# Where operands lie in SBUF: places of weight sets, turned probabilities and raw weights in a one-layer encoder

## The chip, the cores and the metric

The kernel runs on one core of a Trainium2 chip. The metric is the device time of one execution in microseconds. Three runs of the kernel before took 1039.4, 1039.71 and 1041.84 us; the median is 1039.71.

## The reference

One layer of an encoder works on 512 tokens of width 1024, in float32: a SwiGLU feed-forward block (width 2816), two attention mixers side by side on one normalised input, and a second SwiGLU block. Each of the three has an RMSNorm ahead of it, and shift, scale and gate come from a conditioning vector `c`.

```python
mod = c_act @ w_mod[l] + b_mod[l]
h = modulate(rmsnorm(x, norm_ffn1[l]), sh1, sc1)
x = x + 0.5 * g1 * swiglu(h, w_ffn1_in[l], w_ffn1_out[l])
h = modulate(rmsnorm(x, norm_mix[l]), sh2, sc2)
qa, ka, va, qb, kb, vb, ga, gb = split(h @ w_in[l])
ya = window_gqa_sink(rope(norm(qa)), rope(norm(ka)), va, sink_a) @ w_branch_a[l]
yb = (rmsnorm(diff_attention(qb, kb, vb, lam)) * 0.8) @ w_branch_b[l]
x = x + g2 * ((sigmoid(ga) * ya + sigmoid(gb) * yb) @ w_out[l])
h = modulate(rmsnorm(x, norm_ffn2[l]), sh3, sc3)
x = x + 0.5 * g3 * swiglu(h, w_ffn2_in[l], w_ffn2_out[l])
```

Mixer A is attention in a window of 128 with a sink; mixer B takes the difference of two softmaxes.

## The kernel before

**Precision.** Each float32 matrix is split into a high part in float32r and a low part, the remainder (`split_from`, L189: ScalarE copies, VectorE subtracts). A product is three matmuls, high x high, high x low, low x high (`mm3`, L173 to L175; `two`, L456 to L458, for halves of 256 tokens). Activations lie with features on the partitions, tokens along them.

**Weight sets.** Weights stream from HBM. A load lands in a raw tile (512 KB, 1024 elements per partition), is split into one of `HILO` = 5 sets in the tiles `high` and `low`, and the matmuls read it from there. `high_low` (L193 on) hands out the sets in turn. Set i begins at element i x 1024 + min(i, 2) x GAP + `aside` of the two tiles; a set that a holder still needs is passed over. The aside shifts a set by a few elements: 0, `ASIDE` (16), `TURN` (24) or `FAR` (64), chosen where the load is written.

**SBUF.** Tiles are laid one behind the other in the order in which their tags first appear: the scratch of the DMA descriptors, small tiles, `x`, `high`, `mod` columns, `low`, `begin`, `ka`, twelve `b8` tiles of 8 KB per partition, more `mod` columns, six `u4` tiles of 4 KB, `pos`, five `raw` tiles of 4 KB, eight `f2` tiles of 2 KB.

**The stages.** Up to about 61 us: loads, the first norm, the modulation and the first four blocks of the first feed-forward product. Then two blocks with 512-column matmuls, and the others in units (`Unit`, L460 on): seven products of 256 columns where plain halves take eight, with sums of operands (`n1`, `n2`, `t3`, `t4`) and sums of weights made by accumulating DMAs from the POOL queue. A set of such a unit is 24 matmuls. `n1` of both feed-forward blocks lies in u4 tiles, the other sums in b8 tiles. The output of the first block comes in four chunks (`Out1`) of 512-column matmuls between the units; its last four rows of blocks run in halves of 256 tokens (`by_halves`) in `boundary`, beside which the next norm and the first three gates run. These three gates have their weights in u4 tiles (`spare`).

From about 377 to 700 us the mixers run. A planner (`Line`) puts pieces of the attentions, each with a due time from a written cost, between the main stream's matmuls: `project` for vb, kb, qb, `gates`, `project_pairs` for the a projections (there the weights are streamed and `hh`, `hl` are what is loaded), more gates, then `branch` for w_yb and w_ya. In the attentions the probabilities are turned by TensorE (`turned`), split into u4 tiles (`diff_turn`, `window_turn`) and multiplied with the values as loaded operand. `load_main` fetches a set through a raw tile: SP issues the load, ScalarE makes the high copy and a negated one, and POOL adds the weights to the latter by an accumulating DMA. `load_halves` splits with `split_from`. w_out follows (`MIX_ASIDES`), then `in_unit` and `out_unit` for the second feed-forward block: a plain unit, a leading unit that runs beside it, and the others in a written order (`items`), with the two out units of a part behind each group; of an out unit the sets run as s1, a11, a12, s2, s4, s3, a22, with the set a22 of the unit before between s1 and a11.

**Order.** Inside `manual_schedule` and in the units the order on each engine is the written one; elsewhere the tile planner picks by priority. SP and POOL issue transfers in order, so a transfer that waits for its tile holds up those behind it.

Of the kernel before, what the change touches and what calls it, by code (L numbers as in the profile page):

```python
# [98 lines left out]

ASIDE, TURN, GAP = 16, 24, 64  # L100

FAR = 64


BRANCH_ASIDES = (ASIDE, TURN, ASIDE, ASIDE), (ASIDE,) * 4
MIX_ASIDES = 0, 0, 0, 0, 0, 0, ASIDE, ASIDE

# [26 lines left out]
def layer(ctx: ExitStack, tc: tile.TileContext, a: dict):  # L134
# [13 lines left out]
    def xt():  # L148
        return sbuf("x", [P, T], F32, 8)
# [7 lines left out]
    def u4(dt=F32R):  # L157
        return sbuf("u4", [P, 2, T], dt, 6)
# [7 lines left out]
    def keep(shape, nm, dt=F32):  # L166
        return sb.tile(shape, dt, name=nm, tag=nm, bufs=1)
# [28 lines left out]
    def high_low(n=1024, aside=0, holder=None):  # L196
        while turn[0] % HILO in holders:
            turn[0] += 1
        i = turn[0] % HILO
        turn[0] += 1  # L200
        if holder:
            holders[i] = holder
        i = i * 1024 + min(i, 2) * GAP + aside
        return tuple(t[:, i : i + n] for t in parts)
# [27 lines left out]
    rqa, ccol = keep([P, NT, 8], "rqa"), small(NC)  # L232
    x = [xt() for _ in range(NC)]
    parts, modv = [], []
    for nm, n in (("high", 6), ("low", 0)):
        parts.append(keep([P, HILO * 1024 + 2 * GAP + ASIDE], nm, F32R))
        modv += [keep([P, NC], f"mod{v}") for v in range(n)]
# [13 lines left out]

    begin, begins, norms = keep([P, 6 * NC], "begin"), {}, {SC1: NORM1, SC2: NORM2, SC3: NORM3}

# [206 lines left out]
    class Unit:  # L460
# [14 lines left out]

        in_order = turned = by_columns = ()
        spare, roomy, apart, more = ("s1",), (), (), {"s1": ("s2", "a11"), "s2": ("s4", "a12"), "a11": ("s3", "a21")}
# [16 lines left out]
        def prepare(self, q):  # L494

            if q in self.ready:
                return
            self.ask(q)
            n = self.depth * 2 * P
            if q in self.apart:  # L500
                both = b8().rearrange("p a b -> p (a b)")
                hi, lo = both[:, 0:n], both[:, 1024 : 1024 + n]
            else:
                hi, lo = high_low(n, TURN if q in self.turned else ASIDE, (self, q))
            t = self.at[q]
            with tc.issue_after(copied[0]) if q in self.in_order and copied else nullcontext():
                split_from(hi, lo, t)
            self.ready[q] = hi, lo
            if q in self.more:
                s, src = self.more[q]  # L510
                G.dma_start(t, self.srcs[src], accum_op=ALU.add)
                self.at[s] = t
# [104 lines left out]
    hh, hl = new_h()  # L617
    modv += [keep([P, NC], f"mod{v}") for v in range(len(modv), 9)]
    nc.scalar.dma_start(ccol, a["c"])
    tc.keep_in_program_order(nc.scalar.dma_start(par, a["par"]))  # L620
# [3 lines left out]
    with tc.manual_schedule(engines=BOUND | {mybir.EngineType.SP, mybir.EngineType.Pool}):  # L624
# [24 lines left out]
        def first_loads(k):  # L649
            n = 1 if k else 2  # L650
            scale = mod_load(SC1, k, n=n)
            if k == 0:
                kept.append(keep([P, NT], "pos", I32))
            shift = mod_load(SH1, k, n=n) if k == 0 else None
            raw = sbuf("raw", [P, 1024], F32, RAW)
            load_by(raw, a["w1s"][k], n)
            w1[k] = [scale, shift or mod_load(SH1, k), raw]
# [227 lines left out]
    def in_unit1(p):  # L885
        srcs = {q: a["w1u"][p - PLAIN, i] for i, q in enumerate(("a11", "a12", "a21", "a22"))}
        u = Unit(srcs, 4, h1_operand, in_post1, p % 2)
        u.p, u.in_order = p, ('s2', 's4')
        return u

    class Out1:
# [17 lines left out]
        def prepare(self, m):  # L909
            if m not in self.ready:  # L910
                self.ask(m)
                aside = FAR if not self.by_halves(m) else TURN if m < NC - LAST_1 + 2 else ASIDE
                if self.final and m == 0:
                    while turn[0] % HILO != 1:
                        turn[0] += 1
                t = self.ready[m] = high_low(self.depth * P, aside, (self, m))
                with tc.issue_after(copied[0]):
                    split_from(*t, self.at[m])
# [196 lines left out]
    def load_main(src, aside=0):  # L1115

        raw = sbuf("raw", [P, 1024], F32, RAW)
        nc.sync.dma_start(raw, src)
        hi, lo = high_low(aside=aside)
        halves = slice(0, 512), slice(512, 1024)  # L1120
        for j in halves:
            S.copy(hi[:, j], raw[:, j])
        for j in halves:
            S.activation(lo[:, j], raw[:, j], AF.Identity, scale=-1.0)
        G.dma_start(lo, src, accum_op=ALU.add)
        return hi, lo


    def load_halves(src, aside=0):
        raw = sbuf("raw", [P, 1024], F32, RAW)  # L1130
        hi, lo = high_low(aside=aside)
        nc.sync.dma_start(raw, src)
        for j in (slice(0, 512), slice(512, 1024)):
            split_from(hi[:, j], lo[:, j], raw[:, j])
        return hi, lo
# [61 lines left out]

    def project_pairs(srcs, then):

        n = 2 * P  # L1200
        out = [bank("acc") for _ in range(2)]
        for u, src in enumerate(srcs):
            wh, wl = load_main(src, ASIDE)
            for t in range(NT):
# [22 lines left out]
    def gates(more=lambda: True):  # L1227
        while gate_next[0] < 16 and more():
            j = gate_next[0]
            gate_next[0] += 1  # L1230

            wh, wl = load_main(a["w_gate"][j], ASIDE * (j == EARLY_A))
            out = bank("acc")
# [152 lines left out]
    def diff_turn(h, b, p):  # L1386
# [4 lines left out]
        if i == 0:  # L1391
            pair = [u4().rearrange("p a b -> p (a b)") for _ in range(2)]
            pt_b[g] = [t.rearrange("p (k i q) -> p k i q", k=NT, i=2) for t in pair]
# [228 lines left out]
    def window_turn(b, g, kc, sc):  # L1622
        tag = turn_tag(b, g, kc)
        tp = turned([sc[q][:, kc * P : (kc + 1) * P] for q in (0, 2, 1, 3)], tag)
        pt = u4()
        with tc.high_priority():
# [37 lines left out]

    def branch(w, j0, o_h, o_l, then, load, r=FULL[0], asides=(0, 0, 0, 0)):
        for u in range(4):
# [13 lines left out]
    def main():  # L1680
# [6 lines left out]
        tables_a()  # L1687
        yield from project_pairs([a["w_kva"][u] for u in range(2)], keys_a)
        for g in range(2):
# [22 lines left out]
        for i, r in enumerate(HALVES):  # L1712
            line.drain(lambda: done["a"] >= 2 * i + 2)
            yield from branch(a["w_ya"], 0, *wa["o"], then_b, load_halves, r, BRANCH_ASIDES[i])

# [87 lines left out]
    def out_unit(part, g, final):  # L1803
# [10 lines left out]
        srcs = {q: a["w2o"][g, i][:, r] for i, q in enumerate(("a11", "a12", "a21", "a22"))}  # L1814
        return Unit(srcs, len(part), act_operand, post, g)

# [23 lines left out]
    plain = units[0] = Plain(units[0].srcs, 4, h_operand, None, 0)  # L1840
    plain.turned = ("a11", "a21")
    lead = units[1]
    lead.spare, lead.roomy, lead.apart = ("s1", "a11", "a12"), ("a22",), ("s1", "a12")
    for u in units[1:]:
        u.in_order = ("s2", "s3", "s4", "a22") if u is lead else ("s1", "s2", "s3", "s4", "a22")
    units[2].MAKE = {**Unit.MAKE, "s2": 3}
    lead.tags = {"w": "acc", "v": "tp"}
    with tc.manual_schedule(engines={mybir.EngineType.Pool}):
# [250 lines left out]
```

## Time and profile before

| | |
|---|---|
| median of three runs | 1039.71 us |
| the profiled execution, its own time | 1039.97 us |
| its span in the profile | 1038.2 us |
| TensorE busy | 1030.8 us, 99%, 7346 matmuls |
| weight loads, VectorE, ScalarE, GpSimd busy | 951.1, 786.9, 583.9, 162.5 us |
| granted clock of TensorE | 1.0 in every slice |

In groups of instructions a row gives line, engine, operation, output and inputs (the first input of a matmul is what is streamed, the second what is loaded, buffer numbers left out), shape, count, busy time and the mean duration of one in ns. Matmuls are pipelined: one of 256 columns lasts about 276 ns, but the next starts after some 113 ns. In a timeline the first column is the start in us, the second the duration.

### The profile page before, as it was taken

The numbers are of one execution on the slowest core, as the hardware profiler recorded it, in microseconds if no ns is written. First come the engines' busy times: TensorE is split into PE (matmuls) and PEld (weight loads), VectorE is DVE, ScalarE is ACT, GpSimd is POOL, SyncE is SP. The second block draws the span as 40 slices with busy tenths as digits, with TensorE's granted clock in tenths as the row PEclk, the third lists the DMA queues.
The fourth block names the chain that finished last, engine by engine and source line by source line (L and its number), as shares of the span: only waits on it lengthen the run. The fifth ranks groups of instructions, "written<-read, shape, count | busy, mean of one in ns | idle before, by whom it ended". The sixth has DMA issues, their size and how long they took to land.

```text
span 1038.2 us, 18851 instructions
## 1 busy us (share of the span) xinstructions
PE 1030.8 (99%) x7346; PEld 951.1 (92%) x7346; DVE 786.9 (76%) x1456; ACT 583.9 (56%) x1014; POOL 162.5 (16%) x190
## 2 busy tenths in 40 slices
PE   9999999999999999999999999999999999999998
PEld 7789899899999998899888888989999999999998
DVE  7786667567796679859782598976899777877877
ACT  6665335244364343667785856525867546654553
POOL 1101110110110100543333101001112112112210
PEclk9999999999999999999999999999999999999999
DMA  9977787966884459796737944974498998989974
GB/s 360 356 238 203 233 231 209 257 166 205 253 203 133 152 192 410 236 288 139 186 69 190 254 134 151 364 252 104 94 237 191 243 229 207 224 223 214 211 156 112
DMA packets 70377, 220.92 MB, mean 213 GB/s; under 512 B 8464, under 2 KB 13200, under 8 KB 70288
## 3 DMA queue, kind: packets, MB, share of 16 engines
q1 hardware_dynamic: 47808, 146.52, 39.0%
q0 software_dynamic: 19344, 68.70, 35.9%
q10 hardware_dynamic: 3136, 4.51, 1.2%
q8 instruction: 57, 0.93, 0.3%
q14 instruction: 32, 0.26, 0.1%
HBM read 209.46 MB, written 10.23 MB: 212 GB/s over the span
## 4 chain that ended last, share of the span: by engine, by line
PE 94%; DMA 2%; DVE 2%; ACT 2%; issue 0%; SPq 0%; DVEq 0%; ACTq 0%
PE acc L457 7%; PE acc L458 7%; PE acc L456 7%; PE sc L457 6%; PE sc L458 6%; PE sc L456 6%; PE sc L173 5%; PE sc L174 5%; PE sc L175 5%; PE acc L173 5%; PE acc L175 5%; PE acc L174 5%; PE tp L1270 2%; DMA raw<-w1s 2%; PE acc L1192 2%; PE acc L1194 2%
## 5 line engine op out<-in xcount | busy, mean ns | idle before, releaser
L189 ACT CAST high<-raw 128x1024 fp32r<-128x1024 f32 (+2 forms) x176 | 158.2, 913 | 152.9 <-PE sc L174 40.4
L189 DVE TENSOR_TENSOR low<-raw,high 128x1024 fp32r<-128x1024 f32 (+2 forms) x176 | 183.2, 1050 | 42.1 <-ACT high L189 40.8
L456 PE MATMUL acc<-b,high 128*128 128x256 f32 x508 | 140.9, 277 | 0.0
L457 PE MATMUL acc<-b,high 128*128 128x256 f32 x508 | 140.7, 277 | 0.1
L458 PE MATMUL acc<-b,low 128*128 128x256 f32 x508 | 140.6, 277 | 0.0
L457 PE MATMUL sc<-b,high 128*128 128x256 f32 x500 | 138.2, 276 | 0.0
L456 PE MATMUL sc<-b,high 128*128 128x256 f32 x500 | 138.1, 276 | 0.0
L458 PE MATMUL sc<-b,low 128*128 128x256 f32 x500 | 138.1, 276 | 0.0
L189 ACT CAST high<-u 128x1024 fp32r<-128x1024 f32 (+1 forms) x73 | 75.5, 1035 | 50.5 <-PE sc L174 20.2
L189 DVE TENSOR_TENSOR low<-u,high 128x1024 fp32r<-128x1024 f32 (+1 forms) x73 | 87.6, 1200 | 20.4 <-ACT high L189 18.8
L173 PE MATMUL sc<-b,high 128*128 128x512 f32 (+1 forms) x272 | 97.5, 358 | 0.0
L174 PE MATMUL sc<-b,high 128*128 128x512 f32 (+1 forms) x272 | 97.2, 357 | 0.0
L175 PE MATMUL sc<-b,low 128*128 128x512 f32 (+1 forms) x272 | 97.1, 357 | 0.0
L457 PEld LDWEIGHTS acc<-b,high 128*128 128x128 f32 x508 | 95.5, 188 | 0.4 <-DVE b L1883 0.3
L456 PEld LDWEIGHTS acc<-b,high 128*128 128x128 f32 x508 | 95.5, 188 | 0.3 <-ACT f L534 0.2
L458 PEld LDWEIGHTS acc<-b,low 128*128 128x128 f32 x508 | 95.4, 188 | 0.0
L458 PEld LDWEIGHTS sc<-b,low 128*128 128x128 f32 x500 | 93.9, 188 | 0.0
L456 PEld LDWEIGHTS sc<-b,high 128*128 128x128 f32 x500 | 93.9, 188 | 0.0
L457 PEld LDWEIGHTS sc<-b,high 128*128 128x128 f32 x500 | 93.9, 188 | 0.0
L173 PE MATMUL acc<-b,high 128*128 128x512 f32 (+1 forms) x240 | 89.0, 371 | 0.0
L175 PE MATMUL acc<-b,low 128*128 128x512 f32 (+1 forms) x240 | 86.7, 361 | 0.0
L174 PE MATMUL acc<-b,high 128*128 128x512 f32 (+1 forms) x240 | 86.5, 361 | 0.0
(397 smaller groups left out, 2715.9 us busy)
## 6 DMA issues: line engine op xcount, KB each, us to landing
u<-w_mod SPq DMA_DIRECT2D x38, 512.0 KB, 8.3
b<-w_mod SPq DMA_DIRECT2D x32, 512.0 KB, 5.5
raw<-w2i SPq DMA_DIRECT2D x31, 512.0 KB, 5.4
u<-w2i POOLq DMA_DIRECT2D x31, 512.0 KB, 6.7
raw<-w1u SPq DMA_DIRECT2D x24, 512.0 KB, 7.1
u<-w1u POOLq DMA_DIRECT2D x24, 512.0 KB, 7.1
raw<-w1o SPq DMA_DIRECT2D x24, 384.0 KB, 4.4
raw<-w_gate SPq DMA_DIRECT2D x16, 512.0 KB, 5.2
```

The lines of the kernel that those rows point to most:

```text
L173: PE.matmul(out, wh, xh, start=first, stop=False)
L174: PE.matmul(out, wh, xl, start=False, stop=False)
L175: PE.matmul(out, wl, xh, start=False, stop=last)
L189: last = S.copy(hi, src), V.tensor_tensor(lo, src, f(hi), ALU.subtract)
L456: PE.matmul(out, wh[:, s], xh, start=first and j == 0, stop=False, skip_group_check=True)
L457: PE.matmul(out, wh[:, s], xl, start=False, stop=False, skip_group_check=True)
L458: PE.matmul(out, wl[:, s], xh, start=False, stop=last and j == 1, skip_group_check=True)
L1192: PE.matmul(out[t][:, 0:n], hh[k][:, ht], wh[:, o : o + n], start=k == 0, stop=False)
L1194: PE.matmul(out[t][:, 0:n], hl[k][:, ht], wh[:, o : o + n], start=False, stop=k == NC - 1)
L1270: PE.transpose(tp[:, j * P : (j + 1) * P], src, ident)
```

## The change

It moves operands within SBUF and swaps two kinds of tiles; no matmul, no split and no transfer is added or removed.

- `high_low`: every set is followed by GAP (64 elements), and 16 elements are added to every aside. `TURN` goes; `FIRST` = -8 and `ENTRY` = 32 are new.
- Two unused tiles, `pad1` (48 elements) ahead of `high` and `pad2` (40) ahead of u4; `begin` and `pos` become longer. The descriptor scratch shrinks from 4096 to 2048 bytes, since the sets take more.
- Single sets stand at FIRST: the first set behind an Out1 chunk or at the start of the units, one of the last w_out sets, units[2]'s a11, s1 of the first out unit of a part (not the last part), the first w_ya set. In project_pairs the first set has aside 8 (-FIRST), the others -16. Of the last Out1 rows in halves the first stands at ENTRY.
- Gates from `EARLY_A` (5) on have aside -16.
- `load_main`, and `load_halves` where it is given an aside (w_ya), take their raw weights into u4 tiles; the turned probabilities of both attentions go into raw tiles.

```diff
-ASIDE, TURN, GAP = 16, 24, 64
+ASIDE, FIRST, GAP = 16, -8, 64
+ENTRY = 32
-BRANCH_ASIDES = (ASIDE, TURN, ASIDE, ASIDE), (ASIDE,) * 4
-MIX_ASIDES = 0, 0, 0, 0, 0, 0, ASIDE, ASIDE
+MIX_ASIDES = 0, 0, 0, 0, 0, 0, FIRST, ASIDE
...
-        i = i * 1024 + min(i, 2) * GAP + aside
+        i = i * (1024 + GAP) + ASIDE + aside
...
+    keep([P, 48], "pad1")
-        parts.append(keep([P, HILO * 1024 + 2 * GAP + ASIDE], nm, F32R))
+        parts.append(keep([P, HILO * (1024 + GAP) + ASIDE], nm, F32R))
...
-    begin, begins, norms = keep([P, 6 * NC], "begin"), {}, {SC1: NORM1, SC2: NORM2, SC3: NORM3}
+    begin, begins, norms = keep([P, 6 * NC + ASIDE], "begin"), {}, {SC1: NORM1, SC2: NORM2, SC3: NORM3}
...
-                hi, lo = high_low(n, TURN if q in self.turned else ASIDE, (self, q))
+                hi, lo = high_low(n, self.asides.get(q, ASIDE), (self, q))
...
+    keep([P, 40], "pad2")
...
-                kept.append(keep([P, NT], "pos", I32))
+                kept.append(keep([P, 2 * NC], "pos", I32)[:, 0:NT])
...
+        if p == PLAIN:
+            u.asides = {"s1": FIRST}
+        elif 2 * p in [c.start for c in CHUNKS[1:]] or p == PLAIN + 1:
+            u.asides = {"s2": FIRST}
...
-                aside = FAR if not self.by_halves(m) else TURN if m < NC - LAST_1 + 2 else ASIDE
+                aside = (ENTRY if m == NC - LAST_1 else ASIDE) if self.by_halves(m) else FAR
...
     def load_main(src, aside=0):
-        raw = sbuf("raw", [P, 1024], F32, RAW)
+        raw = u4(F32).rearrange("p a b -> p (a b)")
...
-    def load_halves(src, aside=0):
-        raw = sbuf("raw", [P, 1024], F32, RAW)
+    def load_halves(src, aside=None):
+        if aside is None:
+            raw, aside = sbuf("raw", [P, 1024], F32, RAW), 0
+        else:
+            raw = u4(F32).rearrange("p a b -> p (a b)")
...
-            wh, wl = load_main(src, ASIDE)
+            wh, wl = load_main(src, -FIRST if first else -ASIDE)
+            first = False
...
-            wh, wl = load_main(a["w_gate"][j], ASIDE * (j == EARLY_A))
+            wh, wl = load_main(a["w_gate"][j], -ASIDE if j >= EARLY_A else 0)
...
-            pair = [u4().rearrange("p a b -> p (a b)") for _ in range(2)]
+            pair = [sbuf("raw", [P, 1024], F32R, RAW) for _ in range(2)]
...
-        pt = u4()
+        pt = sbuf("raw", [P, 1024], F32R, RAW).rearrange("p (a b) -> p a b", a=2)
...
-            yield from branch(a["w_ya"], 0, *wa["o"], then_b, load_halves, r, BRANCH_ASIDES[i])
+            yield from branch(a["w_ya"], 0, *wa["o"], then_b, load_halves, r, (ASIDE if i else FIRST,) + (ASIDE,) * 3)
...
-        return Unit(srcs, len(part), act_operand, post, g)
+        u = Unit(srcs, len(part), act_operand, post, g)
+        if g == 0 and not final:
+            u.asides = {"s1": FIRST}
+        return u
...
-    plain.turned = ("a11", "a21")
...
+    units[2].asides = {"a11": FIRST}
...
-    nc = bacc.Bacc("TRN2", target_bir_lowering=False, num_devices=1, dynamic_dma_scratch_size=4096)
+    nc = bacc.Bacc("TRN2", target_bir_lowering=False, num_devices=1, dynamic_dma_scratch_size=2048)
```

More of the change, by code (lines that the diff above doesn't have):

```diff
@@ L474, in layer @@
         asked, length = ("s1", "a11", "a12", "a22"), 1.0
-        in_order = turned = by_columns = ()
+        in_order, by_columns, asides = (), (), {}
         spare, roomy, apart, more = ("s1",), (), (), {"s1": ("s2", "a11"), "s2": ("s4", "a12"), "a11": ("s3", "a21")}
@@ L1196, in project, with project_pairs @@
         then(out)
-    def project_pairs(srcs, then):
+    def project_pairs(srcs, then, first=False):
         n = 2 * P
@@ L1662, in window_out, with branch @@
             turns["w"] = (b, g * nk + kc + 1)
-    def branch(w, j0, o_h, o_l, then, load, r=FULL[0], asides=(0, 0, 0, 0)):
+    def branch(w, j0, o_h, o_l, then, load, r=FULL[0], asides=(0,) * 4):
         for u in range(4):
@@ L1687, in main @@
         tables_a()
-        yield from project_pairs([a["w_kva"][u] for u in range(2)], keys_a)
+        yield from project_pairs([a["w_kva"][u] for u in range(2)], keys_a, True)
         for g in range(2):
```

## The prediction

> **What bounds the kernel now.** I read the page's busy times first, then what TensorE waited for, then the groups of its instructions by form, over the run and in short windows.
>
> ```profile
> span 1038.2 us, 18851 instructions
> PE 1030.8 (99%) x7346; PEld 951.1 (92%) x7346; DVE 786.9 (76%) x1456; ACT 583.9 (56%) x1014; POOL 162.5 (16%) x190
> PEclk9999999999999999999999999999999999999999
> ```
> ```profile
> PE acc L703 <- ACT b L690: 2.1, 2, 1.7
> PE acc L631 <- DVE sm L637: 0.9, 1, 0.9
> PE tp L728 <- DVE f L718: 0.5, 1, 0.5
> PE acc L186 <- DVE u L189: 0.2, 1, 0.2
> ```
>
> TensorE is busy 99% at the full granted clock, and the second view says that in the whole run it waited 3.7 us for other engines, all but 0.2 us of it before the long stream begins. So the time is the number of matmuls times their spacing, and an edit counts only if it changes the spacing or makes a new wait. The change touches no matmul: their number and shapes stay. What it moves is where operands lie. I call the byte address of an operand modulo 256 its place, worked out from the order and sizes of the allocations: b8 and ka at 64, u4 at 160, raw and f2 at 192, the weight sets (high, low) at 64 plus four times the aside, so 128 with ASIDE, 160 with TURN. The distance is the place of the weights that are being loaded minus that of the operand that is streamed meanwhile. First, does the spacing depend on it? Two windows of the same instructions at the same places (weights 128, b8 at 64, distance 64), before and after a short stop at 315.5 us; columns are window, length, busy time and (x) those reaching into it:
>
> ```profile
> 298.90:315.40 16.50, 16.50 (x148) 1.00 0.71 169
> 316.00:323.40 7.40, 7.40 (x65) 1.00 0.54 159
> ```
> ```profile
> L456 PE MATMUL acc<-b,high 128*128 128x256 f32 x62 | 17.1, 276 | 0.0
> ```
> ```profile
> L457 PE MATMUL acc<-b,high 128*128 128x256 f32 x22 | 6.2, 281 | 0.0
> ```
>
> About 2.4 more reach into a window than start in it, so the spacing is 16.50/145.6 = 113.3 ns before the stop and 7.40/62.6 = 118.2 ns after it. The mean of one (276 in the window 797.5 to 825, 281 in 316.2 to 323.4) moves by the same 5 ns. So mean ns above 276 is a price per 256-column matmul, and distance 64 has two paces, a quick one and a slow one, that last until something disturbs them. The other distances, each a group by form:
>
> ```profile
> L458 PE MATMUL acc<-u,low 128*128 128x256 f32 x80 | 22.4, 280 | 0.0
> ...
> L457 PE MATMUL acc<-u,high 128*128 128x256 f32 x80 | 22.3, 279 | 0.0
> L456 PE MATMUL acc<-u,high 128*128 128x256 f32 x80 | 22.3, 279 | 0.0
> ...
> L457 PE MATMUL sc<-u,high 128*128 128x256 f32 x72 | 20.1, 280 | 0.0
> L458 PE MATMUL sc<-u,low 128*128 128x256 f32 x72 | 20.1, 280 | 0.0
> L456 PE MATMUL sc<-u,high 128*128 128x256 f32 x72 | 20.1, 279 | 0.0
> ```
> ```profile
> L456 PE MATMUL acc<-b,high 128*128 128x256 f32 x8 | 2.2, 281 | 0.0
> ```
> ```profile
> L456 PE MATMUL acc<-b,b 128*128 128x256 f32 x8 | 2.3, 283 | 0.0
> ```
>
> The 456 with u4 (distance 224) cost 3 to 4 ns each. The fourth group is the 24 that follow the 512-column matmuls of an Out1 (window 142.56 to 145.3): distance 64 in its slow pace. The last is distance 0: 7 ns.
>
> **The change part by part.** The new layout, by the same arithmetic: the scratch gives back 2048 bytes, a multiple of 256; pad1 puts high and low at place 0, GAP between all sets keeps each there, pad2 puts u4 at 64, the longer pos puts raw and f2 at 128; b8 and ka stay at 64. A set then stands at 64 (aside 0), 128 (ASIDE), 32 (FIRST), 192 (ENTRY) or 0 (-ASIDE). Pads, begin and pos issue nothing and cost nothing.
>
> 1. The u4 operands get distance 64. Now 80 x (4+3+3) + 72 x (4+4+3) = 1.59 us. Of these the PLAIN unit's 24 in s1 and 48 in s1 of two out units stand at place 32, distance 224 as now, 72 x 3.5 = 0.25. I take the quick pace for the rest, since the window 797.5 to 825 and its like hold it for long. Saved: **1.34**. At worst they run at 281 and 0.5 is lost.
>
> 2. The three leading sets after an Out1 go from 281 to the 280 of distance 224: 72 x 1 = **0.07**; the u4 set behind them, counted in 1, no longer has to disturb the slow pace.
>
> 3. In project_pairs the weights are what is streamed, and hh and hl are loaded.
>
> ```profile
> L1211 PE MATMUL acc<-high,b 128*128 128x256 f32 x21 | 5.9, 280 | 0.0
> L1213 PE MATMUL acc<-high,b 128*128 128x256 f32 x21 | 5.9, 279 | 0.0
> ```
> These 288 (window 455 to 462, distance 192) go to distance 64, the first set to 224: between 0 (slow pace, no better) and 288 x 3.3 = 0.95. Transposes and scores break in here, and after a break either pace may come, so I take a third: **0.3**.
>
> 4. Turned probabilities, with vb or vz as the weights (window 500 to 645):
>
> ```profile
> L175 PE MATMUL acc<-b,low 128*128 128x512 f32 x119 | 46.8, 393 | 0.0
> L174 PE MATMUL acc<-b,high 128*128 128x512 f32 x119 | 46.6, 392 | 0.0
> ...
> L175 PE MATMUL op<-u,b 128*128 128x256 f32 x64 | 18.1, 282 | 0.0
> L174 PE MATMUL op<-u,b 128*128 128x256 f32 x64 | 18.0, 281 | 0.0
> ```
> In raw (place 128) they get distance 192, whose rows are those of point 3: 216 x (281.5 - 279.5) = **0.43**. Ends: 0, and 216 x 5.5 = 1.19 if distance 192 has a quick pace too.
>
> 5. The 11 gates from EARLY_A on, 264 matmuls of 512 columns, go from distance 0 to 192, which no 512-column row shows. The undisturbed ones at distance 0 (window 377 to 428), and those at distance 64 (502.2 to 506.6):
>
> ```profile
> L1192 PE MATMUL acc<-high,b 128*128 128x512 f32 x58 | 22.6, 389 | 0.0
> ```
> ```profile
> L174 PE MATMUL acc<-b,high 128*128 128x512 f32 x7 | 2.8, 395 | 0.0
> ```
> Now they take 392.5 in the attention (389 only in long runs). Ends: 264 x 3.5 = 0.92 gained, 264 x 2.5 = 0.66 lost. 392.5 itself lies about midway, so I take **0**.
>
> 6. The boundaries (windows 340 to 377 and 701 to 746.2).
>
> ```profile
> L174 PE MATMUL acc<-b,u 128*128 128x256 f32 x48 | 13.5, 280 | 0.0
> ```
> ```profile
> L174 PE MATMUL sc<-b,high 128*128 128x256 f32 x48 | 13.4, 280 | 0.0
> ```
> ```profile
> L456 PE MATMUL sc<-b,high 128*128 128x256 f32 x40 | 11.1, 278 | 0.0
> ...
> L174 PE MATMUL sc<-b,high 128*128 128x256 f32 x32 | 9.0, 280 | 0.0
> ```
> The first three gates' weights in u4 come to distance 0 from 96: 144 x (283 - 280) = 0.43 **lost**. The last Out1 and w_mix (144 and 96 at 280) get one set at 192 or 32 and the rest at 128; after stops both paces occur, so of 240 x 4 = 0.96 I take a quarter, 0.24. FFN2's plain unit leaves TURN: of 120 x 2 = 0.24 half, 0.12; w_ya the same kind, 0.05. Together **0.0**.
>
> 7. Buffers. w_gate, w_yb, w_kva, w_qa and w_ya now pass through u4 (6 tiles, shared with the a tables, the mask and mod columns), the probabilities through raw (5 tiles, with the b tables until the keys and queries are done). SP issues in order: behind a load that waits for a u4 tile stand the next weights and the gate_scr reads, for which TensorE and then DVE wait. Past the start TensorE waits 0.2 us in all (the fourth row of the second view), so sets arrive ahead of their use now, and that lead covers the swap; I take 0. If it is gone, each late set shows as a wait of TensorE for high or low. No row shows what the halved scratch could hold back; the transfers that POOL issues make TensorE wait nowhere now, so 0.
>
> Sum: 1.34 + 0.07 + 0.3 + 0.43 + 0 + 0 = 2.1 us. The profiled run took 1039.97, so 1037.9; the median, 1039.71, lies 0.26 lower: about **1037.6**.
>
> **The rivals.** *The quick pace holds almost everywhere*: points 1 (1.34), 2, 3 (0.95), 4 (1.19), 5 (0.92), 6 (0.7 instead of 0), and the 65 behind the stop (0.3): 5.4 us, 1034.3; half of what is open gives 1036. For it: the quick pace once found lasts for hundreds of matmuls. Against: distance 0 shows no quick one at 256 columns. *Nothing*: the excess belongs to what went before (512 columns, stops), not to places; points 3 to 5 at their low ends and u4 at 281 give -0.5 to +1.3 us, 1038.4 to 1040.2. The Trainium skill is on this side: TensorE: Matmul & The Clock Gate, Step-by-step, gives the streamed and the loaded operand two independent read ports, and SBUF — State Buffer, SBUF: two separate sides, says TensorE never waits on anyone. By that every distance would cost alike and the time would stay 1039.7; the 276, 280 and 283 above disagree. *Slower*: the u4 sets were what threw the slow pace off again. With nearly all of FFN2 at distance 64, one stop puts it there until the next set at 32. The last two of these are s1 of the first out unit of a group; s2, which begins with operands in ka, is the fourth set after it, 4 x 24 x 113.3 ns = 10.9 us later:
>
> ```profile
> 824.80 0.28 PE L456 MATMUL acc<-ka,high 128*128 128x256 f32 x1
> ```
> ```profile
> 939.55 0.28 PE L456 MATMUL acc<-ka,high 128*128 128x256 f32 x1
> ```
> So they stand near 814 and 929 us. Between them lie 1014 matmuls, behind the second up to 1034 us 930: at 4.9 ns 5.0 and 4.6 us. Both lost give 1047.2; it decides from 1060 slow ones, (2.1 + 3.1)/0.0049. For it: the stop at 315.5. Against: at the same instructions now the quick pace lasts. *Earlier start*: TensorE's one long wait stands behind a transfer.
>
> ```profile
> 13.84 10.90 DMA raw<-w1s
> 24.79 0.94 issue
> ```
> If transfers into u4 and raw run quicker from their new places, up to the whole 2.1 us of L703 goes, 1035.5. The Trainium skill, DMA: Bandwidth & Descriptors, How a descriptor splits into AXI transactions, counts the bytes from the 256-byte boundary below the start: a 4096-byte row would take 130 beats instead of 133 in u4, 132 instead of 134 in raw, an estimate of 2%, or 0.3 us of the 16 us up to 24.8; no row here separates it.
>
> **How the numbers follow.** A measurement of this kernel tells about 0.3%, 3.1 us, from no change: faster is below 1036.6, slower above 1042.8. Chances: the forecast 0.46 (1036.4 to 1038.6, of which 0.04 below 1036.6), quick almost everywhere 0.28 (1034 to 1036.5), nothing 0.16, slower 0.06, earlier start 0.04. So faster 0.36, same 0.58, slower 0.06. Leaving out the slower case and the outer parts of two others gives 1034.4 to 1040.3.
>
> **What would show it.** Right: acc<-u and sc<-u at 276 to 277 where they stand at 280 or 279, L1211 to L1213 below 280, the probabilities (now from raw) at 279 to 280, the first gates' acc<-b,u at 283, no new row among TensorE's waits. Wrong: u4 groups at 281; long runs of FFN2 at 281; gates of the attention at 395; a wait of TensorE for high or low.

## The result, and the profile after

Over 21 runs the kernel after takes 1042.25 us (median; 1040.0 to 1046.36), the kernel before, over as many, 1039.77 us (1039.32 to 1041.84). The ratio is 1.0021, with a 95% interval of 1.0014 to 1.0029. The forecast was 1037.6 us and a range of 1034.4 to 1040.3: the change made the kernel 2.5 us slower where 2.1 us less was expected. The size lies within the 0.3% that counted as no change; the sign is certain. The profiled execution took 1042.5 us, against 1039.97 us of the profiled one before, so the two traces differ by what the medians differ by.

The first view is the page's head and busy times, of the kernel after.

```profile
span 1040.7 us, 18847 instructions
PE 1030.6 (99%) x7346; PEld 949.9 (91%) x7346; DVE 787.2 (76%) x1456; ACT 583.9 (56%) x1014; POOL 163.5 (16%) x190
PEclk9999999999999999999999999999999999999999
```

TensorE's busy time is 0.2 us *less* than before (1030.8), the clock is full, and the span is 2.5 us longer. So the time went into gaps between matmuls. The second view, what TensorE waited for (total, times, longest), has them:

```profile
PE acc L705 <- ACT b L692: 1.6, 2, 1.3
PE acc L1221 <- ACT f L1150: 1.5, 1, 1.5
PE acc L173 <- ACT f L1301: 1.2, 1, 1.2
PE acc L633 <- DVE sm L639: 0.9, 1, 0.9
PE tp L730 <- DVE f L720: 0.3, 1, 0.3
PE sc L174 <- DVE b L189: 0.2, 1, 0.2
PE acc L186 <- DVE raw L189: 0.2, 1, 0.2
```

L705, L633, L730 and L186 are the four rows of before under their new line numbers. L1221, L173 and L174 are new: 2.9 us in three waits, none of them for a set of weights (high or low). The first two are for a bank of PSUM, acc, that ScalarE had not yet emptied. A wait also costs the run-up of the stream. From start to start of the matmuls around them, against the same matmuls of run 1 below, which has the same places, the losses are 1.80 us (matmuls 2700 to 2800, about 443 and 447 us), 1.81 us (2800 to 2900, about 462 us) and 0.51 us (at 676 us, in the w_mix stage): 4.1 us.

The third view, groups of TensorE by form, shows what the places did.

```profile
L457 PE MATMUL acc<-u,high 128*128 128x256 f32 x80 | 22.1, 276 | 0.0
...
L459 PE MATMUL acc<-u,low 128*128 128x256 f32 x80 | 22.1, 276 | 0.0
...
L458 PE MATMUL sc<-u,high 128*128 128x256 f32 x72 | 19.9, 277 | 0.0
...
L174 PE MATMUL acc<-b,u 128*128 128x256 f32 x48 | 13.6, 283 | 0.0
```
```profile
L1223 PE MATMUL acc<-high,b 128*128 128x256 f32 x96 | 26.6, 277 | 0.0
```
```profile
L175 PE MATMUL op<-raw,b 128*128 128x256 f32 x64 | 17.9, 279 | 0.0
```

These are the prediction's own signs: u4 operands at 276 to 277, project_pairs below 280, probabilities at 279, the first gates at 283. So the places did what they should, and beside the waits one thing spoils the gain. In windows of FFN2 (length, TensorE's busy time and how many matmuls reach in):

```profile
756.20:769.50 13.30, 13.30 (x120) 13.30 (x119) 12.33 (x19) 9.74 (x16) 2.60 (x3) 1.00 0.99 214
770.20:814.50 44.30, 44.30 (x379) 44.30 (x378) 40.89 (x67) 31.16 (x52) 7.83 (x9) 1.00 0.91 219
```

With the prediction's reading (2.4 more reach in than start) the first window has a spacing of 13.30/117.6 = 113.1 ns, the second 44.30/376.6 = 117.6 ns. The quick pace ends at 769.8 us, at a matmul that opens a new bank and is 11 ns late, and the slow one lasts to 814.9 us, where a set at place 32 (FIRST) comes, distance 224: some 380 matmuls at 4.4 ns, 1.7 us.

Where the 1042.5 - 1039.97 comes from, worked out from the starts of all matmuls in both traces: waits +4.1, the slow pace in FFN2 +0.85 net of what its u4 operands gained, FFN1 -1.0, project_pairs -0.8, probabilities -0.5, the rest about -0.2 together.

Why ScalarE is late is to be read at the three queues. First the loads (SP's queue in time: start, length of the issuing, line, load, count), after and then before. A group's length counts the time the queue stood at a load whose tile was not free.

```profile
415.59 1.53 SPq L1124 DMA_DIRECT2D u<-w_gate  x2
430.83 0.33 SPq L1472 DMA_DIRECT2D u<-table_scr  x1
432.91 5.31 SPq L1124 DMA_DIRECT2D u<-w_kva  x2
439.10 5.64 SPq L1124 DMA_DIRECT2D u<-w_qa  x4
```
```profile
416.67 0.33 SPq L1462 DMA_DIRECT2D u<-table_scr  x1
421.66 10.53 SPq L1118 DMA_DIRECT2D raw<-w_kva  x2
433.95 6.60 SPq L1118 DMA_DIRECT2D raw<-w_qa  x4
```

The table, w_kva and w_qa start 14, 11 and 5 us later than before. Then ScalarE, after and before; the bracket is its idle time and what ended it:

```profile
441.24 1.14 ACT L1128 CAST high<-u 128x512 fp32r<-128x512 f32 x2 [8.35 <-DMA u<-w_kva]
...
442.81 0.56 ACT L1301 COPY f<-acc 128x512 f32<-128x512 f32 x1
...
447.86 0.59 ACT L1301 COPY f<-sc 128x512 f32<-128x512 f32 x1
...
459.09 0.60 ACT L1150 ACTIVATE f<-acc 128x512 f32<-128x512 f32 x1 [0.91 <-DVE rqb L1257]
```
```profile
439.10 0.56 ACT L1291 COPY f<-acc 128x512 f32<-128x512 f32 x1
...
443.62 0.57 ACT L1291 COPY f<-sc 128x512 f32<-128x512 f32 x1
...
454.71 0.60 ACT L1141 ACTIVATE f<-acc 128x512 f32<-128x512 f32 x1 [0.91 <-DVE rqb L1247]
```

ScalarE stands 8.35 us at its copy of w_kva, and the copies of the finished queries out of the banks (L1301, before L1291) are queued behind it: the first is 3.7 us late, the last 4.2. VectorE's rotation of the queries starts late by as much, and the end of a gate (L1150), which follows it in ScalarE's queue, comes 4.4 us late. The first of these keeps L173 waiting for a bank, the last L1221.

### The profile page after: what moved, and what is told of

It is laid out like the page before. It is cut to its first block, busy times and chain, and to the rows that moved or that the text cites. A ratio compares the mean times of both kernels' runs of the same rounds, so it can differ in the third digit from the quotient of the medians.

```text
span 1040.7 us, 18847 instructions
## 1 busy us (share of the span) xinstructions
PE 1030.6 (99%) x7346; PEld 949.9 (91%) x7346; DVE 787.2 (76%) x1456; ACT 583.9 (56%) x1014; POOL 163.5 (16%) x190
## 4 chain that ended last, share of the span: by engine, by line
PE 89%; DVE 4%; DMA 3%; ACT 2%; issue 1%; POOL 1%; SPq 0%; DVEq 0%; ACTq 0%; POOLq 0%
PE acc L458 7%; PE acc L457 7%; PE acc L459 7%; PE sc L458 6%; PE sc L459 6%; PE sc L457 6%; PE sc L174 5%; PE sc L175 5%; PE sc L173 5%; PE acc L173 4%; PE acc L175 4%; PE acc L174 4%; PE tp L1280 2%; DMA raw<-w1s 2%; PE sc L186 2%; PE acc L1203 1%
## 5 line engine op out<-in xcount | busy, mean ns | idle before, releaser
L189 ACT CAST high<-raw 128x1024 fp32r<-128x1024 f32 (+2 forms) x160 | 148.5, 944 | 144.8 <-PE sc L174 44.5
L189 DVE TENSOR_TENSOR low<-raw,high 128x1024 fp32r<-128x1024 f32 (+2 forms) x160 | 172.2, 1087 | 40.1 <-ACT high L189 38.9
L189 ACT CAST high<-u 128x1024 fp32r<-128x1024 f32 (+2 forms) x89 | 85.2, 959 | 59.8 <-PE sc L174 20.2
L189 DVE TENSOR_TENSOR low<-u,high 128x1024 fp32r<-128x1024 f32 (+2 forms) x89 | 98.6, 1108 | 21.9 <-ACT high L189 20.3
L174 PE MATMUL sc<-b,high 128*128 128x512 f32 (+1 forms) x272 | 97.2, 357 | 0.2 <-DVE b L189 0.2
L173 PE MATMUL sc<-b,high 128*128 128x512 f32 (+1 forms) x272 | 97.2, 358 | 0.0
L173 PE MATMUL acc<-b,high 128*128 128x512 f32 (+1 forms) x240 | 89.2, 372 | 1.2 <-ACT f L1301 1.2
L174 PE MATMUL acc<-b,high 128*128 128x512 f32 (+1 forms) x240 | 86.5, 360 | 0.0
```

The costliest lines, as they stand in the source:

```text
L173: PE.matmul(out, wh, xh, start=first, stop=False)
L174: PE.matmul(out, wh, xl, start=False, stop=False)
L189: last = S.copy(hi, src), V.tensor_tensor(lo, src, f(hi), ALU.subtract)
```

## The experiments

Two theories were set against each other. **A**: the swap of tiles (raw weights to u4, probabilities to raw) makes the new waits, and the places save what was forecast. **B**: the places themselves cost, or the slow pace does. Unless said otherwise an experiment is an edit of the kernel after; the ratios are to the kernel before, each with its 95% interval.

**1. The places alone.**

```
 def load_main:    raw = sbuf("raw", ...)      # was u4(F32)
 def load_halves:  raw = sbuf("raw", ...)      # was u4(F32)
 diff_turn:        pair = [u4() ... for _ in range(2)]   # was sbuf("raw", ...)
 window_turn:      pt = u4()                             # was sbuf("raw", ...)
```

> The kernel after, with only its buffers put back: the raw weights of project_pairs, the gates, w_yb and w_ya load into raw again, and the probabilities of both attentions are split into u4 again. All places of the sets stay as the kernel after has them. Theory A (the swap of tiles made the new waits of TensorE at 443, 447, 462 and 676 us in the trace of the kernel after, 4.2 us more than before, and the places by themselves save): the stretch from matmul 2700 to 2900 loses its 3.6 us of waits, the probabilities give back about 0.7, and the time is 1037.5 to 1039.2, faster than the kernel before. Rival B (the moved places, not the tiles, reorder the work and make the waits): waits of that size stay and the time stays at 1041 to 1043. Rival C (only the slow pace in FFN2 costs): the time stays above 1041 by the same amount whether the waits go or not.

Measured: 1037.89 us, ratio 0.9981 (0.9971 to 0.9991). TensorE's waits:

```profile
PE acc L705 <- ACT b L692: 2.0, 2, 1.7
PE acc L633 <- DVE sm L639: 0.9, 1, 0.9
PE acc L186 <- DVE u L189: 0.2, 1, 0.2
```

All three new waits are gone, and the trace has no slow stretch from 765 us on. Theory A holds, and this is the forecast's 1037.6 to within 0.3 us (its terms fit less well, see below). B falls as the cause of the loss. Run 1 keeps the halved descriptor scratch and the pads, so these cost nothing that shows.

**2. The swap alone**: the kernel before with the four edits of the first experiment made the other way round.

> The kernel before, with only the buffers changed as the change has them: raw weights of project_pairs, gates, w_yb and w_ya through u4, probabilities of both attentions in raw. All old places of the sets stay. Theory A (the swap makes the waits): 4.2 us of new waits less 0.7 us of faster probabilities, 1042 to 1045, slower than the kernel before by 2 to 5 us. Rival B (the places make the waits): within 1 us of the kernel before, 1038.7 to 1040.5.

Measured: 1044.76 us, ratio 1.0041 (1.0029 to 1.0053). Its waits have the same two rows, by its own line numbers:

```profile
PE acc L1214 <- ACT f L1144: 1.5, 1, 1.5
...
PE acc L173 <- ACT f L1294: 0.4, 1, 0.4
```

So the swap costs 0.41%, or 4.3 us, with the old places (3.0 to 5.5 by the interval, from five executions); with the new ones it costs 1.0021 - 0.9981, 0.40%. Within these intervals the two parts of the change add up, and the waits come with the old places too. Not all of this trace's excess is the swap's: at matmul 200 it is already 1.6 us behind the trace of before, in the start-up, long before the tiles that the swap moves; it loses 2.9 us between matmuls 2700 and 2900.

**3. Only project_pairs' raw weights back in raw**, the probabilities in raw too.

> The kernel after, with the raw weights of project_pairs alone (w_kva and w_qa, six loads) back in raw; gates, w_yb, w_ya stay in u4 and the probabilities in raw. Theory A1 (the waits at 443 and 462 us come from w_kva and w_qa standing in line for u4 tiles behind modulation columns and the table): both go, 3.1 to 3.5 us less than the kernel after, 1038.5 to 1039.5. Rival A2 (raw is now the short kind, since the differential attention's probabilities hold it at the same time): other waits of 1 us and more show in 425 to 475 us and the time is 1041 or more.

Measured: 1049.44 us, ratio 1.0090 (1.0077 to 1.0104): far worse, rival A2. SP's queue and the largest wait:

```profile
434.42 43.59 SPq L1124 DMA_DIRECT2D u<-w_gate  x7
478.10 0.86 SPq L1124 DMA_DIRECT2D raw<-w_qa  x2
```
```profile
PE acc L1222 <- DMA low<-w_qa: 3.4, 1, 3.4
```

The last two loads of w_qa leave at 478.1 us where the kernel after has issued all four by 444.7: in SP's queue they stand behind seven loads of gates into u4 tiles, which take 43.6 us. Between 482 and 501 us 10.8 us are lost against the trace of before, later than A2 said. That they were put so far back because raw's five tiles were taken by the differential attention's probabilities fits A2, but no view shows it. Which loads stand in line in u4 is what the next runs ask.

**4. More sets at place 32 in FFN2**, instructions and order unchanged.

```
 units[2].asides = {"a11": FIRST}
+for u in units[3:]:
+    u.asides = {"s1": FIRST}
```

> The kernel after, with every unit of FFN2 from the fourth on (8 of 11) taking its s1 set at place 32 (FIRST) instead of 64, so that at least one set in seven can end a slow pace. The order of the instructions is the same. Theory D (a hitch of some ns puts TensorE into the slow pace of 118 ns, which lasts until a set at place 32; the trace of the kernel after has it from 769.8 to 815 us for 1.6 us, and other executions have it elsewhere): 8 such sets cost 0.08 each, 0.65 in all, the slow stretches are cut to one unit (0.8 us) at most, the median falls by 0.3 to 1.0 us and the spread of the runs is less. Rival E (the spread comes from the waits on transfers, not from the pace): the median rises by the 0.65 and the spread stays.

Measured: 1041.53 us, ratio 1.0010 (1.0001 to 1.0018); lowest to highest 2.7 us, the kernel after 6.4 over more runs. The ratio is 1.1 us below that of the kernel after, in the direction of theory D and at its upper bound, but the two intervals overlap. The profiled execution, at 1040.3 us the fastest of the eleven, doesn't decide it either: at 768.5 us, where the slow pace of the kernel after began, its matmuls come 0.26 us late and then go on in the quick pace, so the first added set, at 774 us, had no slow pace to end. Runs 10 and 11 decide.

**5. Two gates' raw weights out of u4**: in the kernel after, the table and w_kva start just when ScalarE has copied these.

```
-wh, wl = load_main(a["w_gate"][j], ...)                  # u4
+wh, wl = load_main(a["w_gate"][j], ..., j < EARLY_A)     # True: raw
```

> The kernel after, with the raw weights of two gates alone (the third and fourth of the late ones, loaded before EARLY_A) back in raw; all else as after, TensorE's order the same. In the trace of after these two hold u4 tiles until ScalarE has copied them at 430.7 and 432.8 us, and the table that is loaded next waits until 430.8 us (416.7 before), w_kva behind it until 432.9 and 437.9, and ScalarE stands 8.4 us at its copy of w_kva with the copies out of acc queued behind it. Theory A1 (that chain is the cause of the waits at 443 and 462 us): the table loads by 418 us, w_kva by 425, both waits of TensorE shrink below 0.5 in sum, and the time is 1038.3 to 1039.8, 2.5 to 3.6 less than after. Rival A2 (the differential attention's demand on raw, or the order of ScalarE's work, makes them): the time stays above 1041.5 with waits of over 2.5 in that stretch.

Measured: 1042.55 us, ratio 1.0020 (1.0011 to 1.0029): no better. Its queue and its wait:

```profile
415.49 0.33 SPq L1472 DMA_DIRECT2D u<-table_scr  x1
416.69 18.47 SPq L1124 DMA_DIRECT2D u<-w_kva  x2
437.75 3.95 SPq L1124 DMA_DIRECT2D u<-w_qa  x4
```
```profile
PE acc L1221 <- ACT f L1150: 3.2, 1, 3.2
```

The table is on time now, and the first wait (443 us) is gone, but SP stands at the second w_kva until about 435 and then at w_qa; ScalarE stops later, at w_qa, and the wait at 462 us doubles. My A1 took the first link of the line for the whole. What holds the other tiles is seen on VectorE in the same trace:

```profile
436.43 1.28 DVE L282 CUSTOM_DVE_ANT_0 u<-u,ka,par 128x1024 f32<-128x1024 f32 x1
...
440.05 1.28 DVE L282 CUSTOM_DVE_ANT_0 u<-u,ka,par 128x1024 f32<-128x1024 f32 x1
```

These are the first and the last of four modulation columns. Their loads into u4 were issued by about 413 us, and they are computed only after the rotation of the keys, and w_qa's loads leave from the end of the first of them on (437.75). In the first experiment they run at the same time and harm nothing, since no weights of a projection need their tiles.

**6. The table in b8** instead of u4.

```
-late = u4(F32).rearrange("p a b -> p (a b)")
+late = b8(F32).rearrange("p a b -> p (a b)")[:, 0:1024]
 nc.sync.dma_start(late, table_scr)
```

> The kernel after, with only the table of the window attention's rotations loaded into the first half of a b8 tile instead of a u4 tile, so that the raw weights of w_kva take the u4 tile that the table waited for. Theory A1: w_kva loads one tile earlier, at 430.8 and 432.9 us instead of 432.9 and 437.9, ScalarE's stand of 8.4 us falls to about 4, the wait at 443 (1.2 to 1.4 us) goes and that at 462 (1.7) halves or more: 1039.5 to 1041. Rival A2: the waits stay, 1041.5 to 1043.

Measured: 1044.26 us, ratio 1.0039 (1.0025 to 1.0053): a miss. w_kva issues at 430.6, as expected, and the wait at 443 is halved (0.6 us), but that at 462 grows (2.8 us for L1221, 1.5 after), as in run 5. The profiled execution also waits 0.7 us for L535's copy in FFN2; whether the rest of its 1044 is of that kind stays open.

**7. The gates' places**, on the kernel of experiment 1: aside 0 for all late gates instead of -16. (Aside 0 is place 64 and so distance 0; the 208 below is a slip.)

> The kernel of the first run (buffers put back, places of after), with every late gate's set at place 16 + 0 again, distance 208 to the 512-column operands' place 64, in place of aside -16. Nothing else is changed in the source. Theory F (the gates' places save what the trace of the first run shows, 0.7 us from 463 to 500 us, and not the probabilities' buffers): the time rises by 0.4 to 1.0 to 1038.3 to 1038.9, and the groups of the gates in the two attentions take 2 to 4 ns longer. Rival G (the place of the gates is worth nothing, as the prediction had it): within 0.3 us of the first run, 1037.6 to 1038.2.

Measured: 1037.69 us, ratio 0.9976 (0.9967 to 0.9985). Rival G: the gates' places are worth nothing that can be told, as point 5 of the prediction had it. What the first run saved between 463 and 500 us was project_pairs.

**8. The swap from the window attention on**, undone before it.

> The kernel after, with the swap of tiles kept only from the window attention on (its probabilities in raw; the gates beside it, w_yb and w_ya through u4) and put back for the differential attention (probabilities in u4; project_pairs and the gates beside it through raw). Theory A: the waits at 443 and 462 us go, that at 676 us (0.2 to 0.5) may stay; 1037.3 to 1039. Rival H (the meeting of both ways where the window attention begins makes a wait of its own at 470 to 500 us): 1039 to 1042, with that wait in the trace.

Measured: 1045.73 us, ratio 1.0043 (1.0026 to 1.0059). The waits at 443 and 462 us are gone, so it is the swap's part beside the differential attention that makes them. But rival H holds, at another place than it gave: a new wait where the window attention starts its turns, 6.8 us more than in the kernel after from start to start between 567 and 637 us. (One of the seven executions took 4233 us, for a reason that isn't known; the ratio is without it.)

```profile
PE tp L1280 <- DVE b L189: 3.7, 1, 3.7
```

So half the swap is no better than the whole. Whether the window attention's half would cost anything without the border isn't shown: the kernel after, which swaps on both sides, has no wait of that size there.

**9. The four columns first.**

```
-mod_col(*asked.pop(0), ...)
+with tc.high_priority(AHEAD) if columns is later and len(asked) + len(columns) <= 4 else nullcontext():
+    mod_col(*asked.pop(0), ...)
```

> The kernel after, with only the last four modulation columns (L282) given priority, so that VectorE computes them some 35 of its instructions earlier, ahead of the rotation of the differential attention's keys, and not at 436.6 to 441.4 us. Until they are computed they hold four of the six u4 tiles. Theory A3 (the tiles that w_kva and w_qa wait for are those of these four columns: in the fifth run the loads of w_qa follow the columns' ends at 437.8, 439.0, 440.2 and 441.4 one by one): the loads of w_kva and w_qa issue 4 us or more earlier, the waits at 443 and 462 us fall from 3.6 to under 1.5 in sum and the time is 1038.6 to 1040.6. Rival A2 (ScalarE's order with the copies of raw weights ahead of the copies out of acc makes the waits by itself, whenever the loads land): the waits stay above 2.5 and the time is above 1041.3.

Measured: 1040.59 us, ratio 1.0001 (0.9991 to 1.0011), 2.1 us below the kernel after (1.0021) by the ratios, with intervals that don't meet. The queue and the waits:

```profile
422.99 0.33 SPq L1473 DMA_DIRECT2D u<-table_scr  x1
424.79 3.48 SPq L1125 DMA_DIRECT2D u<-w_kva  x2
429.75 7.51 SPq L1125 DMA_DIRECT2D u<-w_qa  x4
```
```profile
PE acc L457 <- ACT f L535: 1.3, 1, 1.3
PE acc L1203 <- DVE low L189: 1.1, 2, 0.7
```

The loads leave 8 to 9 us earlier, and the wait at 462 us (1.81) is gone, and L173's for L1301. But 1.6 us are still lost between matmuls 2700 and 2800: TensorE now waits 1.1 us in the projection before, L1203, for VectorE to split weights: the columns now stand ahead of that split. So A3 is right about the tiles, and moving the columns only moves a part of the price. This trace is of the slowest of the twelve executions (1043.63 us): 1.1 us of its excess over the trace of before arise in the start-up, 1.5 at the wait for L535 in FFN2, which comes and goes (0.7 us in run 6, 0 in run 1) and is not of this stage, and 0.8 net behind that wait, where a slow stretch begins.

**10. Four more sets at place 32**, on the kernel of experiment 7.

> The kernel of the seventh run (buffers put back, gates' sets at 16), with the s1 sets of every second unit of FFN2 from the fourth on (4 of 11) at place 32 (FIRST). The order of all instructions is the same. Theory D (a slow pace, entered at some hitch, lasts until a set at place 32): 4 x 0.08 = 0.3 us of cost against slow stretches that end sooner; within 0.3 us of the seventh run's ratio of 0.9976, and a spread between lowest and highest of less than its 2.8 us. Rival E (spread from the start-up's transfers): 0.3 us slower than the seventh run, spread unchanged.

Measured: 1037.70 us, ratio 0.9977 (0.9968 to 0.9986), lowest to highest 2.9 us: in the time no difference from run 7. Its trace shows what the added sets do. At 765.5 us, at the same matmul as in the kernel after, the opening of a bank comes 84 ns late and the slow pace begins; the first added set comes 48 matmuls later, at 771.2 us, and behind it the pace is quick, 5.40/45.6 = 118 ns before and 34.50/304.6 = 113.3 ns after:

```profile
765.70:771.10 5.40, 5.40 (x48) 5.40 (x48) 4.73 (x6) 4.51 (x7) 0.14 (x1) 1.00 0.98 244
774.50:809.00 34.50, 34.50 (x307) 34.50 (x306) 32.57 (x57) 25.13 (x43) 6.09 (x7) 1.00 0.92 208
```

In the kernel after, without such a set there, the slow pace lasted some 380 matmuls. The swap isn't in this kernel, so the slow pace isn't the swap's doing. What such a set saves where it is needed and what it costs elsewhere come out even here.

**11. No sets at place 32 in the FFNs**, on the kernel of experiment 7: `units[2].asides`, out_unit's and in_unit1's asides are left out. No instruction and no order changes, only where seven sets lie: at place 128, which is distance 64, instead of 32. (The "64" below, and that in experiment 4, is the distance.)

> The kernel of the seventh run, with all leading sets of the two FFNs' units (FIRST at place 32, asides of in_unit1, units[2] and out_unit) back at 64. The order of all instructions is the same. Theory D: nothing is left that ends a slow pace between 260 and 365 us and between 733 and 1035 us but chance; what is saved is 7 sets x 0.08 = 0.6 us, what is risked is 4.44 ns for each of up to 2600 matmuls, 11 us: the trace shows groups of u4 and b operands at 280 to 281 over long stretches where the seventh run's show 276, and the median rises by 1 to 8 us with a wider spread. Rival E (the pace heals by itself, or the sets at 32 have nothing to do with it): 0 to 0.6 us faster than the seventh run.

Measured: 1053.32 us, ratio 1.0123 (1.0107 to 1.0140), 15.6 us slower than run 7. The largest group, without and with those sets:

```profile
L457 PE MATMUL acc<-b,high 128*128 128x256 f32 x508 | 142.9, 281 | 0.0
```
```profile
L457 PE MATMUL acc<-b,high 128*128 128x256 f32 x508 | 140.8, 277 | 0.0
```

And in a long window of FFN2 without them, 210.00/1783.6 = 117.7 ns:

```profile
820.00:1030.00 210.00, 210.00 (x1786) 210.00 (x1785) 154.13 (x228) 115.99 (x171) 36.56 (x43) 1.00 0.85 198
```

With them it is 208.00/1834.6 = 113.4 ns between 817 and 1025 us. Theory D is shown for the two FFNs, and its price was set too low: FFN1 is slow as well (5.2 us more than in run 7 between 87 and 330 us, 10.8 in FFN2). Left at distance 64 and without a break, the stream did not find the quick pace again, in FFN2 over some 2500 matmuls. A break can restore it: in FFN1, behind a stop of 0.25 us at 319.7 us, the last 66 matmuls are quick, 7.10/62.6 = 113.4 ns. In the kernel before, the stop at the same matmul (315.5 us) ended the quick pace.

```profile
320.30:327.40 7.10, 7.10 (x65) 7.10 (x64) 5.83 (x9) 3.54 (x6) 0.00 (x0) 1.00 0.54 164
```

## Why the prediction was wrong

| step | forecast, us saved | after | run 1 |
|---|---|---|---|
| 1 and 2, u4 operands and leading sets | 1.41 | 0.2 (FFN1 1.0, FFN2 -0.85) | 1.9 |
| 3, project_pairs | 0.30 | 0.8 | 0.7 |
| 4, probabilities | 0.43 | 0.5 | 0.2 |
| 5, late gates | 0 | 0.1 | 0.1 |
| 6, boundaries | 0 | 0.1 | -0.2 |
| 7, buffers | 0 | -4.1 | 0 |

(The columns after and run 1 are sums over each group's matmuls of the distance from its start to the next start, less 113.3 ns at 256 columns and 226.7 at 512, against the trace before; row 7 is the waits. Steps 1 and 2 can't be told apart so, and FFN2 is taken from 767 us on.)

*Step 7 failed.* "Past the start TensorE waits 0.2 us in all ..., so sets arrive ahead of their use now, and that lead covers the swap; I take 0." The row said that TensorE does not wait for sets, and that is still so: it waits for none in the kernel after. What the step left out is the engine between. ScalarE copies the raw weights *and* empties the banks, in one order; a late raw tile stops it at the copy of w_kva for 8.35 us, and the queries' copies behind it have no lead of that size. The step named who shares u4 (the table, the mask, the modulation columns) but did not look up until when: the four columns hold two thirds of it from 413 to 441 us, and w_kva and w_qa are due from 421 us on in the trace before. Both times stand in the trace of before. The swap costs 4.3 us (runs 1 and 2), twice the forecast's whole gain. The sign that I gave, a wait of TensorE for high or low, was the wrong one too; it was a wait for acc, released by ScalarE.

*The rival "slower" was half right.* Its mechanism, that u4 operands at distance 224 had thrown the slow pace off and nothing near does so now, is what the trace shows at 769.8 to 814.9 us and run 11 shows in the large. Its place (behind 814 and 929 us) and its need (1060 slow matmuls to turn the sign) were off: 380 came, 1.7 us, and without the waits they would have left a gain. The same stretch is slow in the traces of runs 8 and 9 and quick in those of runs 3 to 6, so with the same places it comes in some executions and not in others. Its 0.06 was too low for a mechanism that one late bank can start.

*Point 1* had the right size wherever the quick pace holds: 1.9 us with the leading sets in run 1, 1.41 forecast, and 0.3 of the 1.9 are the 65 matmuls behind the stop at 315.5 us, which the forecast counted only in a rival. *Point 3* was sized too low: project_pairs is quick after most interruptions, not after one in three; in the kernel after 189 of its 288 matmuls are followed within 115 ns. So run 1 meets the forecast's total in part by luck: in its trace points 1 to 3 saved more than forecast and point 4 less. *Point 4* has the right size, but 0.3 of its 0.5 needs the swap that costs 4.3; with the probabilities in u4 (run 1) 0.2 is left. *Points 5 and 6* came out as forecast, within 0.3 us; the first gates are at 283 as said. (Point 5's 389 ns at distance 0 are L1192, a line of the projections, where the weights are streamed, and not gates.) *The rival "nothing"*, by which places don't count (its -0.5 to +1.3 us leave out point 5's low end, -0.66), falls with run 11: seven sets moved by 96 bytes, with no instruction changed, make 15.6 us. The Trainium skill (TensorE: Matmul & The Clock Gate, Step-by-step) gives the streamed and the loaded operand independent read ports; by that rule run 11 would have taken run 7's time. *"Earlier start"*: at 87 us the traces of after and before stand within 0.04 us of each other; L705's wait is 1.6 us in the kernel after but 2.0 in run 1, whose tiles lie at the same places, against 2.1 before. In the eleven traces with the new places matmul 400 (87 us) comes between 0.7 us earlier and 1.1 later than before, in run 2, with the old ones, 1.6 later. So no gain is shown. The prediction's 0.3 us, which takes a rule on the bytes that a transaction fetches for one on the place it writes to, could not be told from this spread either.

*A version that beats both* is the change without its swap: run 7 at 0.9976 and run 1 at 0.9981 of the kernel before, 1037.7 to 1037.9 us, with intervals that meet each other and not 1.

What stays open: how the slow pace begins. In FFN2 it began at the same matmul in the traces of the kernel after and of runs 8, 9 and 10, where a bank opens at 765 to 773 us, which in run 9 waits for L535's copy: 11 ns late in the kernel after, 50 in run 8, 84 in run 10, 1.5 us in run 9. In runs 3 to 7 the matmuls there came 0.05 to 0.26 us late and the pace stayed quick, so the length of the delay alone doesn't decide it. Open too are what makes this wait come and go, how often the executions of the kernel after are slow there, and how the 4.1 us divide between the table, the gates and the columns, since runs 5, 6 and 9 each removed one wait and lengthened or made another.

## What to carry to other kernels

When a buffer is moved to another pool, list who holds that pool's tiles at that hour and until when, and then what is queued on the copying engine behind the copy that will wait: the price shows at a bank or an operand of quite another stage, not at the moved buffer. When a layout is tuned to a pace that can be lost, see to it that something restores it, and price the loss by the number of matmuls until then. Two ideas in one change should be built apart: here one was worth +2 us and the other -4.3.

## What was not expected of the hardware

The spacing of 256-column matmuls at distance 64 has two lasting values, 113.4 and 117.7 ns, and in the FFNs 24 matmuls at distance 224 bring the quick one back: after the three Out1 chunks of the kernel before, at 815 us in the kernel after, at 771 us in run 10. Without such sets, in run 11, the slow one lasts through FFN2 and nearly all of FFN1, 15.6 us in a kernel of 1037. It is no rule for every stream: in project_pairs of run 7 (weights streamed) 48 matmuls stand at distance 224, and the 30 behind them at distance 64 are slow (117.8 ns) until the second break. The quick one, a mean of 276 ns, is also below what the other distances show: 283 at distance 0, 280 at 224, 279 at 192.
